# Packing the chunk operands of two RWKV heads into common tiles, with three scalings on another engine and more products of zeros at the start

## The chip, the cores and the metric

The kernel runs on one core of a Trainium2 chip. The metric is the time of one execution on the device in microseconds (us). A run is given as the median of several executions; the profile comes from one execution, taken by the hardware profiler.

## The reference, cut to what matters

The program is two layers of a decoder trunk on 256 tokens of width 1024. Each layer has a differential-attention branch and an RWKV-7 branch (8 heads of 64), then an output projection, a SwiGLU feed-forward part and a gated embedding. The change lies in the RWKV branch, whose core is a recurrence over tokens:

```
def step(state, inp):
    r_t, w_t, k_t, v_t, a_t, b_t = inp
    sa = jnp.einsum('bhvk,bhk->bhv', state, a_t)
    state = (state * w_t[:, :, None, :] + sa[..., None] * b_t[:, :, None, :]
             + v_t[..., None] * k_t[:, :, None, :])
    return state, jnp.einsum('bhvk,bhk->bhv', state, r_t)
...
yr = rwkv7_scan(rh, heads(decay), kh, vh, -kk, kk * ah)
```

All values are float32.

## The kernel before, in words

The kernel works in a transposed layout: channels lie on the 128 partitions, tokens along the free axis. Two heads of 64 channels share the 128 partitions, so a tensor of 512 channels is four pairs j (0 to 3) with heads e = 0 (partitions 0 to 63) and e = 1 (64 to 127). The 256 tokens of the recurrence are cut into four chunks c of 64, which makes 16 combinations of j and c.

**Two streams of work.** `main_g` is a generator with the layer's large products: the input projection, whose weights come by DMA and are split into a high part `wh` (ScalarE, L110) and a low part `wl` (VectorE, L111), the attention and its projection. The RWKV part is written out beside it and calls `fill(t)`, which lets `main_g` go on for an amount of TensorE time t taken from a table by name (`FP0`, `FP1`). The large products so stand between the small ones on TensorE, in an order fixed before the run. Tiles of one kind come from pools; the pool of 4 KB tiles (`slot`) holds NSLOT of them.

**The stage that makes the operands (L663 to L724).** From the decay come `Pd` and `Pi`. `NK` (L664) holds, for each j and c, two blocks of 64 columns: the scaled removal keys and the scaled keys. `RA` holds the removal vectors and the receptances; there are four such tiles, one for each head e and two pairs, and only 64 of the 128 partitions of each are written here (L677 to L679). L712 multiplies NK by RA for each head, 128x128 per chunk (the Gram products). Of each result, three pieces go by ScalarE to `AT` and `L2` (L720, L721), and two masked pieces by VectorE: one into the other 64 partitions of the `RA` tile (L722), one into `RK` (L723). The `SV` tile of a head holds the state on its own 64 partitions and the values v on the other 64 (L738), so that one product of 128 rows (L843) sums both. `UV` holds the solved updates and the values. `NT` is the transposed `NK` (L744, L745).

**The triangular solve (L765 to L828).** VectorE inverts the diagonal 16x16 blocks; the result is spread over the partitions by masks `p0` and `p1` into `ex` (L804, L805), transposed on VectorE (L806) and used in 64 + 64 small products (L818).

**The recurrence (L838 to L886).** For each chunk: `pz` (L843), products with the solve's blocks (L854, L861, L867), each followed by copies, then the new state (L876, L884, L885). After every second chunk come the outputs: L898 with the state, L903 with `RK` and `UV`.

**The start (L228 to L243).** NWARM products of zeros run on TensorE while the first inputs are loaded.

Matmuls of float32 are issued as two passes, so their counts in the trace are twice those of the code; transposes are one pass.

Of the kernel before, what the change touches and what calls it, by code (L numbers as in the profile page):

```python
# [25 lines left out]
NSLOT = 27  # L26
# [4 lines left out]
NWARM = 11  # L31
# [26 lines left out]
def trunk(ctx: ExitStack, tc: tile.TileContext, x_in, p_in, ws, par, lora, cst, fin, relb, onehot, out):  # L58
# [19 lines left out]
    def slot8(shape, dt=F32, s="s8"):  # L78
        return sp.tile(shape, dt, tag="s8", bufs=1, name=nm(s))
# [287 lines left out]
    def layer(l):  # L367
# [295 lines left out]
        RA = [[slot([P, 8, P], F32, "RA") for _ in range(2)] for _ in range(2)]  # L663
        NK = slot8([P, 16, 2, 64], F32, "NK")  # L664
# [3 lines left out]
        V.scalar_tensor_tensor(out=NK[:, :, 0], in0=pt16(nb), scalar=-0.5, in1=pt16(Pi), op0=ALU.mult, op1=ALU.mult)  # L668
        fill(fp['pre'])
        V.tensor_mul(NK[:, :, 1], pt16(kp), pt16(Pi))  # L670
        fill(fp['pre'])
        for jp in range(2):
            js = slice(2 * jp, 2 * jp + 2)
            for e in range(2):
                h = half[e]
                ra = RA[e][jp]
                A.copy(ra[h, :, 0:1], pt16(kn[:, js])[h, :, 0:1])  # L677
                V.tensor_mul(ra[h, :, 1:64], pt16(kn[:, js])[h, :, 1:64], pt16(Pd[:, js])[h, :, 0:63])
                V.tensor_mul(ra[h, :, 64:128], pt16(zr[:, js])[h], pt16(Pd[:, js])[h])  # L679
                fill(fp['pre'])  # L680
# [13 lines left out]
        RK = [slot([P, 16, 64], F32, "RK") for _ in range(2)]  # L694
# [8 lines left out]
        def mask4(h, lo):  # L703
            n = h.stop - h.start
            return mg[h, lo:lo + 64].unsqueeze(1).broadcast_to([n, 4, 64])

        for j in range(4):

            pgs = [psax(), psax()]
            for c in range(4):  # L710
                for e in range(2):
                    PE.matmul(pgs[e][:, c * P:(c + 1) * P], NK[half[e], 4 * j + c].rearrange("p a s -> p (a s)"),  # L712
                              RA[e][j // 2][half[e], 4 * (j % 2) + c], start=True, stop=True)
            for e in range(2):
                h, oh = half[e], half[1 - e]
                ra = RA[e][j // 2]
                pg = pgs[e]
                pg3 = pg.rearrange("p (i s) -> p i s", i=4)
                for b in range(2):
                    A.copy(AT[quar[2 * e + b], 4 * j:4 * j + 4], pg3[quar[b], :, quar[b]])  # L720
                A.copy(L2[quar[e], 4 * j:4 * j + 4, quar[e]], pg3[0:32, :, 32:64])  # L721
                V.tensor_mul(ra[oh, 4 * (j % 2):4 * (j % 2) + 4, 0:64], pg3[64:128, :, 0:64], mask4(half[1], 0))  # L722
                V.tensor_mul(RK[e][:, 4 * j:4 * j + 4], pg3[:, :, 64:128], mask4(slice(0, P), 64))  # L723
                fill(fp['g'])  # L724


        SV = [slot([P, 16, 64], F32, "SV") for _ in range(2)]
        UV = [slot([P, 16, 64], F32, "UV") for _ in range(2)]
        NT = [slot([P, 8, P], F32, "NT") for _ in range(2)]
        for tb in range(2):  # L730
# [4 lines left out]
            for r in range(2):  # L735
                c = 2 * tb + r
                for e in range(2):
                    A.copy(SV[e][half[1 - e], c::4], pv4[half[r], :, e])  # L738
                    A.copy(UV[e][64:128, c::4], pv4[half[r], :, e])
            fill(fp['vt'])  # L740
        for i4 in range(4):
            pn = psax()
            for i in range(4):
                PE.transpose(pn[:, i * P:(i + 1) * P], NK[:, 4 * i4 + i].rearrange("p a s -> p (a s)"), ident)  # L744
            A.copy(NT[i4 // 2][:, 4 * (i4 % 2):4 * (i4 % 2) + 4], pn.rearrange("p (i v) -> p i v", i=4))  # L745
            fill(fp['vt'])
# [55 lines left out]
        for tile_, src in ((Ds, DD.rearrange("p t s -> p s t")), (Dt, DD)):  # L802
            ex = tp.tile([P, 16, 32], F32, tag="g2", bufs=3, name=nm("ex"))
            V.tensor_scalar_mul(ex[:, :, 0:16], src, p0)  # L804
            V.tensor_scalar_mul(ex[:, :, 16:32], src, p1)  # L805
# [25 lines left out]
        for e in range(2):  # L831
            G.memset(SV[e][half[e], 0::4], 0.0)
# [5 lines left out]
        for c in range(4):  # L838
            ch = c // 2
            pz = psax()  # L840
            for j in range(4):
# [392 lines left out]
```

## Time and profile before

| what | value |
|---|---|
| runs, median (lowest to highest) | 910.44 us (908.72 to 911.51), 3 runs |
| the profiled execution, whole | 909.44 us |
| its span, first to last instruction | 907.6 us |
| TensorE (PE) busy | 887.8 us |
| VectorE (DVE) busy | 709.6 us |
| ScalarE (ACT) busy | 515.8 us |
| GpSimd (POOL) busy | 18.4 us |

A time measured outside the profiler is compared with the whole time of the profiled execution, which lies 1.84 us over its span. Matmuls are pipelined, and their ends are modelled, so a busy TensorE isn't TensorE at its peak: in a row with many matmuls the time from the start of one to the start of the next says what it costs. PEld is the loading of the stationary operand.

### The profile page before, as it was taken

How to read it: one execution, taken by the hardware profiler on the slowest of the kernel's cores; microseconds unless marked ns; L12 is line 12 of the kernel's file. 1: busy time of each engine (PE TensorE's matmuls, PEld its weight loads, DVE VectorE, ACT ScalarE, POOL GpSimd, SP SyncE). 2: the span in 40 equal slices, each digit the busy share in tenths (PEclk: the TensorE clock that was granted, in tenths of full speed). 3: DMA queues.
4: the chain of work that ended last, by engine and by line, in shares of the span. 5: the costliest groups of instructions: out<-in, count | busy, mean ns of one | idle time of the engine just before them, and what ended most of it. 6: DMA issues, size and time to landing. Idle time of an engine off the chain costs nothing.

```text
span 907.6 us, 17784 instructions
## 1 busy us (share of the span) xinstructions
PE 887.8 (98%) x7011; PEld 800.3 (88%) x7011; DVE 709.6 (78%) x1270; ACT 515.8 (57%) x956; POOL 18.4 (2%) x59
## 2 busy tenths in 40 slices
PE   8999989999999999999999999999999999999996
PEld 7988879899988888889999997989989888888885
DVE  6659977688988888766785996768788888886666
ACT  6475665544555555545567564665465555554444
POOL 0000000100000000000001000000000000000000
PEclk9999999999999999999999999999999999999998
DMA  8563423445666666666554344333665666666661
GB/s 283 190 219 131 140 75 106 126 153 165 208 186 187 188 186 190 198 186 194 170 162 136 107 135 136 95 111 105 185 188 174 195 188 187 190 201 186 192 191 47
DMA packets 42540, 149.47 MB, mean 165 GB/s; under 512 B 4911, under 2 KB 6488, under 8 KB 42328
## 3 DMA queue, kind: packets, MB, share of 16 engines
q1 hardware_dynamic: 41896, 147.87, 53.6%
q8 instruction: 55, 0.90, 0.4%
q10 hardware_dynamic: 560, 0.46, 0.2%
q14 instruction: 29, 0.24, 0.1%
HBM read 147.25 MB, written 2.63 MB: 165 GB/s over the span
## 4 chain that ended last, share of the span: by engine, by line
PE 90%; DVE 6%; ACT 2%; issue 1%; DMA 1%; ACTq 0%; POOL 0%; DVEq 0%; POOLq 0%
PE mm L142 21%; PE mm L128 11%; PE mm L144 10%; PE mm L130 10%; PE mm L129 10%; PE ax L142 8%; PE ax L144 4%; DVE wl L111 2%; ACT wh L110 1%; PE mm L166 1%; PE ax L712 1%; PE mm L167 1%; PE mm L168 1%; PE ax L818 1%; PE ax L843 1%
## 5 line engine op out<-in xcount | busy, mean ns | idle before, releaser
L110 ACT CAST wh<-raw 128x1024 fp32r<-128x1024 f32 (+1 forms) x269 | 280.7, 1046 | 297.0 <-PE mm L142 100.6
L111 DVE TENSOR_TENSOR wl<-raw,wh 128x1024 fp32r<-128x1024 f32 (+1 forms) x269 | 327.3, 1219 | 105.4 <-ACT wh L110 103.9
L128 PE MATMUL mm<-x,wh 128*128 128x256 f32 x704 | 204.1, 290 | 2.1 <-ACT wh L110 1.7
L130 PE MATMUL mm<-x,wl 128*128 128x256 f32 x704 | 202.0, 288 | 0.6 <-DVE wl L111 0.5
L129 PE MATMUL mm<-x,wh 128*128 128x256 f32 x704 | 200.6, 285 | 0.0
L128 PEld LDWEIGHTS mm<-x,wh 128*128 128x128 f32 x704 | 135.0, 192 | 6.2 <-ACT wh L110 2.2
L130 PEld LDWEIGHTS mm<-x,wl 128*128 128x128 f32 x704 | 134.9, 192 | 4.2 <-DVE wl L111 1.6
L129 PEld LDWEIGHTS mm<-x,wh 128*128 128x128 f32 x704 | 135.0, 192 | 1.1 <-issue 0.2
L142 PE MATMUL mm<-f,wh 128*128 128x512 f32 x352 | 97.5, 395 | 0.0
L142 PE MATMUL mm<-x,wh 128*128 128x512 f32 x320 | 87.5, 395 | 0.0
L142 PE MATMUL ax<-x,wh 128*128 128x512 f32 x320 | 87.3, 394 | 0.0
L142 PEld LDWEIGHTS mm<-f,wh 128*128 128x128 f32 x352 | 59.7, 189 | 7.6
L144 PEld LDWEIGHTS mm<-f,wl 128*128 128x128 f32 x352 | 55.1, 189 | 8.1
L142 PEld LDWEIGHTS ax<-x,wh 128*128 128x128 f32 x320 | 54.7, 189 | 7.3
L142 PEld LDWEIGHTS mm<-x,wh 128*128 128x128 f32 x320 | 54.7, 189 | 7.3
L144 PE MATMUL mm<-f,wl 128*128 128x256 f32 x352 | 57.2, 280 | 0.0
L144 PEld LDWEIGHTS ax<-x,wl 128*128 128x128 f32 x320 | 49.1, 189 | 6.8
L144 PEld LDWEIGHTS mm<-x,wl 128*128 128x128 f32 x320 | 49.1, 189 | 6.8
L144 PE MATMUL ax<-x,wl 128*128 128x256 f32 x320 | 50.9, 281 | 0.0
L144 PE MATMUL mm<-x,wl 128*128 128x256 f32 x320 | 50.9, 281 | 0.0
L142 PE MATMUL mm<-m,wh 128*128 128x512 f32 x128 | 35.3, 396 | 0.0
L956 DVE TENSOR_TENSOR xs<-xs,mm 128x256 f32<-128x256 f32 x64 | 26.3, 416 | 9.3 <-PE mm L144 8.7
(293 smaller groups left out, 1385.1 us busy)
## 6 DMA issues: line engine op xcount, KB each, us to landing
raw<-ws SPq DMA_DIRECT2D x267, 512.0 KB, 3.6
lora<-lora SPq DMA_DIRECT2D x2, 768.0 KB, 5.6
vr<-vd SPq DMA_DIRECT2D x1, 1536.0 KB, 9.4
bias<-vr SPq DMA_DIRECT2D x1, 1024.0 KB
out<-y SPq DMA_DIRECT2D x3, 256.0 KB, 2.1
raw<-ws SPq DMA_DIRECT2D x2, 256.0 KB, 4.6
xs<-x_in SPq DMA_DIRECT2D x1, 512.0 KB
pi<-p_in SPq DMA_DIRECT2D x2, 256.0 KB, 3.8
```

Source lines behind the costliest of these rows:

```text
L110: A.copy(wh, raw)
L111: V.tensor_sub(wl, raw, wh.bitcast(F32))
L128: PE.matmul(dst, lh, rh, start=first, stop=False, **kw)
L129: PE.matmul(dst, lh, rl, start=False, stop=False, **kw)
L130: PE.matmul(dst, ll, rh, start=False, stop=last, **kw)
L142: PE.matmul(pm, wh[:, i * P:(i + 1) * P], src[k + i][2], start=k + i == 0, stop=False, skip_group_check=True)
L144: PE.matmul(pm[:, 0:T], wl[:, i * P:(i + 1) * P], src[k + i][0], start=False, stop=k + i == nk - 1, skip_group_check=True)
L166: PE.matmul(dst, x[0][:, tk], wh, start=first, stop=False, skip_group_check=True)
L167: PE.matmul(dst, x[1][:, tk], wh, start=False, stop=False, skip_group_check=True)
L168: PE.matmul(dst, x[0][:, tk], wl, start=False, stop=last, skip_group_check=True)
L712: PE.matmul(pgs[e][:, c * P:(c + 1) * P], NK[half[e], 4 * j + c].rearrange("p a s -> p (a s)"), RA[e][j // 2][half[e], 4 * (j % 2) + c], s ...
L956: V.tensor_add(xs[:, n], xs[:, n], pm)
```

## The change

- `RA` becomes two tiles instead of four; each holds both heads of two pairs on all 128 partitions, made by one operation each instead of one per head.
- `NK` gets a third block, a copy of the first for head 0 (ScalarE), so that head 0 reads its two blocks in the order 1, 2 and head 1 in the order 0, 1.
- The two masked pieces of a Gram result become one operation over 128 columns into a new tile `MK`, and `RK` goes.
- The state lies in one tile `S` for both heads; the values are read from `UV` alone. So `pz` is the sum of two products of 64 rows (RA with S, MK with UV) instead of one of 128; for chunk 0, whose state is zero, only the second. The updates of the state are one operation for both heads.
- `NT` comes from 32 transposes of 64 partitions per layer instead of 16 of 128.
- Three of the four scalings into `ex` go from VectorE to ScalarE.
- 15 products of zeros instead of 11; 26 slots instead of 27; the tile of `NK` grows from 8 KB to 12 KB.

```
-NSLOT = 27
+NSLOT = 26
-NWARM = 11
+NWARM = 15
...
-        RA = [[slot([P, 8, P], F32, "RA") for _ in range(2)] for _ in range(2)]
-        NK = slot8([P, 16, 2, 64], F32, "NK")
+        RA = [slot([P, 8, P], F32, "RA") for _ in range(2)]
+        NK = slot12([P, 16, 3, 64], F32, "NK")
         nb = slot([P, 4, T], F32, "nb")
         V.scalar_tensor_tensor(out=nb, in0=th, scalar=1.0, in1=kn, op0=ALU.add, op1=ALU.mult)
         fill(fp['pre'])
         V.scalar_tensor_tensor(out=NK[:, :, 0], in0=pt16(nb), scalar=-0.5, in1=pt16(Pi), op0=ALU.mult, op1=ALU.mult)
+        A.copy(NK[0:64, :, 2], NK[0:64, :, 0])
+        nk = [NK[half[e], :, 1 - e:3 - e].rearrange("p i a s -> p i (a s)") for e in range(2)]
         fill(fp['pre'])
         V.tensor_mul(NK[:, :, 1], pt16(kp), pt16(Pi))
         fill(fp['pre'])
         for jp in range(2):
             js = slice(2 * jp, 2 * jp + 2)
-            for e in range(2):
-                h = half[e]
-                ra = RA[e][jp]
-                A.copy(ra[h, :, 0:1], pt16(kn[:, js])[h, :, 0:1])
-                V.tensor_mul(ra[h, :, 1:64], pt16(kn[:, js])[h, :, 1:64], pt16(Pd[:, js])[h, :, 0:63])
-                V.tensor_mul(ra[h, :, 64:128], pt16(zr[:, js])[h], pt16(Pd[:, js])[h])
-                fill(fp['pre'])
+            ra = RA[jp]
+            A.copy(ra[:, :, 0:1], pt16(kn[:, js])[:, :, 0:1])
+            V.tensor_mul(ra[:, :, 1:64], pt16(kn[:, js])[:, :, 1:64], pt16(Pd[:, js])[:, :, 0:63])
+            fill(fp['pre'])
+            V.tensor_mul(ra[:, :, 64:128], pt16(zr[:, js]), pt16(Pd[:, js]))
+            fill(fp['pre'])
...
-        RK = [slot([P, 16, 64], F32, "RK") for _ in range(2)]
+        MK = [[slot([P, 8, P], F32, "MK") for _ in range(2)] for _ in range(2)]
...
-                    PE.matmul(pgs[e][:, c * P:(c + 1) * P], NK[half[e], 4 * j + c].rearrange("p a s -> p (a s)"),
-                              RA[e][j // 2][half[e], 4 * (j % 2) + c], start=True, stop=True)
+                    PE.matmul(pgs[e][:, c * P:(c + 1) * P], nk[e][:, 4 * j + c],
+                              RA[j // 2][half[e], 4 * (j % 2) + c], start=True, stop=True)
...
-                    A.copy(AT[quar[2 * e + b], 4 * j:4 * j + 4], pg3[quar[b], :, quar[b]])
-                A.copy(L2[quar[e], 4 * j:4 * j + 4, quar[e]], pg3[0:32, :, 32:64])
-                V.tensor_mul(ra[oh, 4 * (j % 2):4 * (j % 2) + 4, 0:64], pg3[64:128, :, 0:64], mask4(half[1], 0))
-                V.tensor_mul(RK[e][:, 4 * j:4 * j + 4], pg3[:, :, 64:128], mask4(slice(0, P), 64))
+                    A.copy(AT[quar[2 * e + b], 4 * j:4 * j + 4], pg3[quar[2 - 2 * e + b], :, quar[b]])
+                A.copy(L2[quar[e], 4 * j:4 * j + 4, quar[e]], pg3[quar[2 - 2 * e], :, 32:64])
+                V.tensor_mul(MK[e][j // 2][:, 4 * (j % 2):4 * (j % 2) + 4], pg3, mg.unsqueeze(1).broadcast_to([P, 4, P]))
...
-        SV = [slot([P, 16, 64], F32, "SV") for _ in range(2)]
+        S = slot([P, 16, 64], F32, "S")
...
-                    A.copy(SV[e][half[1 - e], c::4], pv4[half[r], :, e])
-                    A.copy(UV[e][64:128, c::4], pv4[half[r], :, e])
+                    A.copy(UV[e][half[e], c::4], pv4[half[r], :, e])
...
-        for i4 in range(4):
-            pn = psax()
-            for i in range(4):
-                PE.transpose(pn[:, i * P:(i + 1) * P], NK[:, 4 * i4 + i].rearrange("p a s -> p (a s)"), ident)
-            A.copy(NT[i4 // 2][:, 4 * (i4 % 2):4 * (i4 % 2) + 4], pn.rearrange("p (i v) -> p i v", i=4))
-            fill(fp['vt'])
+        for jp in range(2):
+            pn = [psax(), psax()]
+            for i in range(8):
+                for e in range(2):
+                    PE.transpose(pn[e][:, i * 64:(i + 1) * 64], nk[e][:, 8 * jp + i], ident[half[e], half[e]])
+            for e in range(2):
+                A.copy(NT[jp][:, :, half[e]], pn[e].rearrange("p (i v) -> p i v", i=8))
+                fill(fp['vt'])
...
-            V.tensor_scalar_mul(ex[:, :, 0:16], src, p0)
-            V.tensor_scalar_mul(ex[:, :, 16:32], src, p1)
+            A.activation(ex[:, :, 16:32], src, AF.Copy, scale=p1)
+            if tile_ is Ds:
+                V.tensor_scalar_mul(ex[:, :, 0:16], src, p0)
+            else:
+                A.activation(ex[:, :, 0:16], src, AF.Copy, scale=p0)
             V.transpose(lanes(tile_), ex)
...
-        for e in range(2):
-            G.memset(SV[e][half[e], 0::4], 0.0)
...
+            if c > 0:
+                for j in range(4):
+                    for e in range(2):
+                        PE.matmul(four(pz)[half[e], j], RA[j // 2][half[e], 4 * (j % 2) + c, 0:64], S[half[e], 4 * j + c],
+                                  start=j == 0, stop=False, skip_group_check=True)
             for j in range(4):
                 for e in range(2):
-                    PE.matmul(four(pz)[half[e], j], RA[e][j // 2][:, 4 * (j % 2) + c, 0:64], SV[e][:, 4 * j + c],
-                              start=True, stop=True)
+                    PE.matmul(four(pz)[half[e], j], MK[e][j // 2][half[e], 4 * (j % 2) + c, 0:64], UV[e][half[e], 4 * j + c],
+                              start=c == 0 and j == 0, stop=j == 3, skip_group_check=True)
...
-                for e in range(2):
-                    h = half[e]
-                    if c > 0:
-                        V.tensor_add(S1[h], four(pS)[h], SV[e][h, c::4])
-                    V.tensor_mul(SV[e][h, c + 1::4], S1[h], PC[h, c::4].unsqueeze(2).broadcast_to([64, 4, 64]))
+                    V.tensor_add(S1, four(pS), S[:, c::4])
+                V.tensor_mul(S[:, c + 1::4], S1, PC[:, c::4].unsqueeze(2).broadcast_to([P, 4, 64]))
...
-                        PE.matmul(four(py[e])[half[cc % 2], j], RK[e][:, 4 * j + cc], UV[e][:, 4 * j + cc],
+                        PE.matmul(four(py[e])[half[cc % 2], j], MK[e][j // 2][:, 4 * (j % 2) + cc, 64:128], UV[e][:, 4 * j + cc],
```

## Rows read from the trace of the kernel before

**Rows 1.** The page's first part: busy us, share of the span, instructions.

```profile
PE 887.8 (98%) x7011; PEld 800.3 (88%) x7011; DVE 709.6 (78%) x1270; ACT 515.8 (57%) x956; POOL 18.4 (2%) x59
```

**Rows 2.** Busy time by stretch: us, engines (instructions), granted clock, DMA share, GB/s.

```profile
71.50:117.68 46.18, 42.72 (x306) 37.74 (x305) 45.05 (x83) 28.08 (x71) 0.94 (x3) 1.00 0.35 108
126.00:200.00 74.00, 73.77 (x865) 67.85 (x862) 54.82 (x118) 42.17 (x102) 3.95 (x8) 1.00 0.36 106
498.00:549.05 51.05, 48.40 (x381) 44.91 (x379) 49.47 (x84) 29.82 (x67) 0.63 (x2) 1.00 0.43 128
```

**Rows 3.** Busy time around the first L818 of either layer, and its timeline.

```profile
115.25:117.68 2.43, 0.28 (x3) 0.10 (x2) 2.43 (x6) 1.38 (x5) 0.00 (x0) 0.99 0.09 12
117.68:121.00 3.32, 3.32 (x135) 3.26 (x136) 3.16 (x6) 1.77 (x4) 0.44 (x2) 0.50 0.70 188
546.59:549.05 2.46, 0.39 (x3) 0.03 (x1) 2.46 (x7) 0.00 (x0) 0.00 (x0) 1.00 0.41 75
...
117.68 1.93 PE L818 MATMUL ax<-D,BT 32*32 32x32 f32 x128 [2.15 <-DVE sm L480]
...
549.05 1.28 PE L818 MATMUL ax<-D,BT 32*32 32x32 f32 x128 [2.07 <-DVE ex L805]
```

**Rows 4.** Chain that ended last, shares by line: 71.5 to 118, then 498 to 550.

```profile
by line: DVE wl L111 20.0%; issue 12.9%; DVE RA L679 5.4%; DVE RK L723 4.7%; DVE p L795 4.5%; DVE RA L678 4.1%; DVE RA L722 3.9%; DVE rk L687 2.8%; DVE kn L653 2.8%; DVE k L536 2.8%; ACT NT L745 2.7%; DVE NK L668 2.6%; DVE bo L755 2.6%; DVE
by line: PE mm L128 18.9%; PE mm L129 18.6%; PE mm L130 18.0%; PE ax L712 12.2%; DVE wl L111 4.5%; ACT SV L738 2.8%; ACT UV L739 2.5%; PE ax L744 2.1%; DVE p L795 2.1%; PE ax L651 2.1%; ACT wh L110 2.0%; DVE D L806 2.0%; ACT AT L720 2.0%; P
```

**Rows 5.** Timeline of VectorE, layer 0, at RA and masks: start us, us, what.

```profile
77.90 0.67 DVE L678 TENSOR_TENSOR RA<-kn,Pd 64x504 f32<-64x504 f32 x1
...
80.52 0.69 DVE L536 SCALAR_TENSOR_TENSOR q<-mm,bc 128x512 f32<-128x512 f32 x1
...
87.69 0.43 DVE L722 TENSOR_TENSOR RA<-ax,cs 64x256 f32<-64x256 f32 x1
...
90.27 0.68 DVE L536 SCALAR_TENSOR_TENSOR k<-mm,bc 128x512 f32<-128x512 f32 x1
```

**Rows 6.** Groups by form: busy us, mean ns; L629: ns least/median/most.

```profile
L755 DVE TENSOR_TENSOR bo<-zv,ax 128x512 f32<-128x512 f32 x4 | 2.7, 680 | 0.0
L804 DVE TENSOR_SCALAR ex<-DD,cs 128x256 f32<-128x256 f32 x2 | 0.8, 391 | 0.0
L720 ACT COPY AT<-ax 32x128 f32<-32x128 f32 x16 | 4.1, 255 | 3.0 <-PE ax L712 2.7
L738 ACT COPY SV<-ax 64x256 f32<-64x256 f32 x16 | 5.9, 368 | 0.2
L629 ACT ACTIVATE kk<-zk,pr x8: 493/497/547, 55.3 to 485.3; 128x256 f32<-128x256 f32 x8
```

**Rows 7.** Timeline of TensorE in the recurrence of layer 0; x counts passes.

```profile
126.47 0.69 PE L843 MATMUL ax<-SV,RA 128*64 128x64 f32 x16
...
129.01 0.68 PE L861 MATMUL ax<-W,L 64*64 64x64 f32 x8
...
147.62 0.68 PE L898 MATMUL ax<-SV,RA 64*64 64x64 f32 x16
148.24 1.15 PE L903 MATMUL ax<-UV,RK 128*64 128x64 f32 x32
```

**Rows 8.** Timeline of TensorE: Gram products of layer 1.

```profile
511.02 2.02 PE L712 MATMUL ax<-RA,NK 64*128 64x128 f32 x16
...
514.59 1.16 PE L712 MATMUL ax<-RA,NK 64*128 64x128 f32 x16
```

**Rows 9.** The start: timeline of TensorE, and busy time by stretch.

```profile
1.19 4.42 PE L233 MATMUL mm<-zw 128*128 128x512 bf16 x11 [1.19 <-DVE zw L230]
7.32 0.38 PE L128 MATMUL mm<-x,wh 128*128 128x256 f32 x1 [1.71 <-ACT wh L110]
...
8.40:11.80 3.40, 3.40 (x18) 3.40 (x17) 3.25 (x7) 3.40 (x8) 0.00 (x0) 0.50 1.04 414
11.80:14.00 2.20, 2.20 (x20) 2.20 (x19) 2.20 (x6) 2.20 (x8) 0.00 (x0) 0.99 1.03 412
```

More of the change, by code (lines that the diff above doesn't have):

```diff
@@ L76, in slot, with slot12 @@
         return sp.tile(shape, dt, tag="s", name=nm(s))
-    def slot8(shape, dt=F32, s="s8"):
-        return sp.tile(shape, dt, tag="s8", bufs=1, name=nm(s))
+    def slot12(shape, dt=F32, s="s12"):
+        return sp.tile(shape, dt, tag="s12", bufs=1, name=nm(s))
     def small(shape, dt=F32, tag="sm", bufs=8):
@@ L701, in layer @@
         mg = cs[:, K_MG:K_MG + P]
-        def mask4(h, lo):
-            n = h.stop - h.start
-            return mg[h, lo:lo + 64].unsqueeze(1).broadcast_to([n, 4, 64])
         for j in range(4):
@@ L711, in layer @@
                 for e in range(2):
-                    PE.matmul(pgs[e][:, c * P:(c + 1) * P], NK[half[e], 4 * j + c].rearrange("p a s -> p (a s)"),
-                              RA[e][j // 2][half[e], 4 * (j % 2) + c], start=True, stop=True)
+                    PE.matmul(pgs[e][:, c * P:(c + 1) * P], nk[e][:, 4 * j + c],
+                              RA[j // 2][half[e], 4 * (j % 2) + c], start=True, stop=True)
             for e in range(2):
[L715 to L718, printed above, removed]
+                pg3 = pgs[e].rearrange("p (i s) -> p i s", i=4)
                 for b in range(2):
-                    A.copy(AT[quar[2 * e + b], 4 * j:4 * j + 4], pg3[quar[b], :, quar[b]])
-                A.copy(L2[quar[e], 4 * j:4 * j + 4, quar[e]], pg3[0:32, :, 32:64])
-                V.tensor_mul(ra[oh, 4 * (j % 2):4 * (j % 2) + 4, 0:64], pg3[64:128, :, 0:64], mask4(half[1], 0))
-                V.tensor_mul(RK[e][:, 4 * j:4 * j + 4], pg3[:, :, 64:128], mask4(slice(0, P), 64))
+                    A.copy(AT[quar[2 * e + b], 4 * j:4 * j + 4], pg3[quar[2 - 2 * e + b], :, quar[b]])
+                A.copy(L2[quar[e], 4 * j:4 * j + 4, quar[e]], pg3[quar[2 - 2 * e], :, 32:64])
+                V.tensor_mul(MK[e][j // 2][:, 4 * (j % 2):4 * (j % 2) + 4], pg3, mg.unsqueeze(1).broadcast_to([P, 4, P]))
                 fill(fp['g'])
-        SV = [slot([P, 16, 64], F32, "SV") for _ in range(2)]
+        S = slot([P, 16, 64], F32, "S")
         UV = [slot([P, 16, 64], F32, "UV") for _ in range(2)]
@@ L863, in layer @@
             for e in range(2):
-                G.tensor_copy(UV[e][0:32, c::4], W1[quar[e]])
+                G.tensor_copy(UV[e][quar[2 - 2 * e], c::4], W1[quar[e]])
             fill(fp['w2'])
@@ L868, in layer @@
                           skip_group_check=True)
-            V.tensor_copy(UV[0][32:64, c::4], four(pw)[quar[2]])
-            A.copy(UV[1][32:64, c::4], four(pw)[quar[3]])
+            V.tensor_copy(UV[0][quar[3], c::4], four(pw)[quar[2]])
+            A.copy(UV[1][quar[1], c::4], four(pw)[quar[3]])
             fill(fp['u'])
@@ L897, in layer @@
                         if cc > 0:
-                            PE.matmul(four(py[e])[half[cc % 2], j], RA[e][j // 2][half[e], 4 * (j % 2) + cc, 64:128],
-                                      SV[e][half[e], 4 * j + cc], start=j == 0, stop=False, skip_group_check=True)
+                            PE.matmul(four(py[e])[half[cc % 2], j], RA[j // 2][half[e], 4 * (j % 2) + cc, 64:128],
+                                      S[half[e], 4 * j + cc], start=j == 0, stop=False, skip_group_check=True)
             for j in range(4):
```

## The prediction

> **What bounds the kernel now.** I read the page first: TensorE is busy for 98% of the span and VectorE for 78% [rows 1], so a TensorE-bound kernel at first sight. The stretches, layer by layer, say more [rows 2]. In the recurrence (126 to 200 us) TensorE is busy for 73.77 of 74 us: what it does there is paid in full, and what VectorE saves there is worth nothing. In the stretch before it, where the chunk operands are made and masked, it is the other way round: in layer 0 (71.5 to 117.68) VectorE is busy for 45.05 of 46.18 us and TensorE idles 3.46; in layer 1 (498 to 549.05) VectorE for 49.47 of 51.05, and TensorE idles 2.65. Most of that idle time lies in one place: before the products of L818 TensorE works 0.28 of 2.43 us in layer 0 and 0.39 of 2.46 in layer 1, while VectorE works all the time [rows 3]: the products wait for the transposed diagonal blocks of `ex`. The chain that ended last shows the same for layer 0, lines of VectorE from one end to the other; in layer 1 it is mixed, with 55% in three lines of TensorE's own products and 5% in ScalarE's copies of `SV` and `UV` [rows 4]. So the change is judged by two sums: what leaves VectorE before L818, and what comes to TensorE in the recurrence.
>
> **The parts that leave VectorE.** `RA`: the four operations of one pair of head pairs took 77.90 to 80.52, 2.62 us [rows 5]. They cover 64 partitions each; afterwards two cover 128 with the same 512 elements in each partition. An operation on 128 partitions and 512 elements took 680 ns (L755) [rows 6], as these do, so half goes: 1.31 us, twice a layer, 2.6 us.
> Masks: six operations took 87.69 to 90.27, 0.43 each [rows 5]; two for each head and group of four chunks, eight times a layer, are 6.9 us. Afterwards one of 128x512 from PSUM: 0.60 to 0.70 by L755's 680 ns, less overlap, 5.2 us. That saves 1.7. But each waits for three copies of ScalarE out of the same bank, 255 ns each (L720; L721's has the same shape) [rows 6], a pace of about 0.8 us: eight times 0.8 is 6.4, and 0.5 is saved. ScalarE can run ahead where VectorE is busy with `RA` and `rk`; I take 1.2.
> Scalings: an `ex` on VectorE takes 0.39 us [rows 6]. Ahead of the first transpose one of two goes to ScalarE, and runs beside the other: 0.35 saved. The second pair goes whole, two at 497 ns (L629's shape) in series on ScalarE; it is needed only for the second set of L818, behind TensorE's other products.
> The Trainium skill, "ScalarE: Activation LUTs", Rules for kernel authors, says of `mul` "Use VectorE, not ScalarE". The rows agree on the price, 497 against 391 ns, but VectorE is what everything waits for here; by the rule the 0.35 would be no saving, and the sum below 0.7 us worse over two layers.
> Together 2.6 + 1.2 + 0.35 = 4.2 us a layer. The bounds: 2.6 + 0.5 = 3.1 if the scalings bring nothing, less 1.2 if the second write of `NK` (VectorE) has to wait for ScalarE's new copy inside the same tile (1024 elements on 64 partitions, an estimate: L738 took 368 ns for 256 [rows 6], four times that is 1.5, and part of it passes while VectorE hands over), so 1.9; and 2.6 + 1.7 + 0.6 = 4.9 above. The trace has no two engines writing interleaved columns of one tile at once, so this wait can't be excluded; behind it on VectorE would stand `RA` and everything after.
>
> **What else is moved, at no cost on the path.** ScalarE gains the `NK` copy (at most 1.5) and three scalings (1.5) and loses eight `SV` copies of 368 ns [rows 6], 2.9 us: about even over a layer, but in layer 1, where these copies are on the chain [rows 4], lighter at the right place. The two memsets of GpSimd on `SV` go. In the recurrence five operations of 0.42 us a layer leave VectorE: hidden under TensorE's work. If that cover were gone they would be a gain, so nothing is risked. The pool has 26 slots for 27, the tiles of this stage 7 (RA 2, MK 4, S 1) for 8: the same room at the peak. `MK` asks for two slots more at its place, but its writer is VectorE, behind the last readers of `kn`, `Pd` and `zr`, which free slots; I take nothing, at worst 1 us.
>
> **What comes to TensorE.** For chunk 0 eight products of K=64 replace eight of K=128. For chunks 1 to 3 there are sixteen instead of eight. A product is two passes. Sixteen passes took 0.69 us with K=128 (L843) and 0.68 with K=64 (L898), 32 took 1.15 (L903) [rows 7]: chunk 0 costs the same, and each other chunk (1.15 - 0.69) = 0.46 more; three a layer, 1.38 us, all of it in the recurrence, where nothing hides it.
> The Gram products (L712) get cheaper. 16 passes took 2.02 us where the two heads' products ran one after the other and 1.16 where they ran side by side on the two halves of the array [rows 8]. Of four groups a layer two ran apart (in layer 0, 77 to 92 us, and in layer 1 alike), since the two `RA` of a pair were made one after the other. With one `RA` both heads are ready together: up to 1.7 us a layer.
> The transposes of `NK` become 32 of 64 partitions for 16 of 128. Side by side the 32 cost about what the 16 did; one after the other they add at most sixteen passes like those of L712 that ran apart (2.02 / 16 = 0.126 us, [rows 8]), 2 us. They lie before L818, where TensorE has slack; I take 0.
>
> **The sum.** In layer 0 TensorE can give 3.46 idle + 1.7 = 5.2, more than VectorE's 4.2: 4.2 is gained. In layer 1 it can give 2.65 + 1.7 = 4.3 and hardly follows; I take 3.8. Together 8.0, less 2 x 1.38 = 2.8: 5.2 us faster.
> Then the start. The 11 products of zeros (4.42 us from 1.19) end at 5.6; TensorE idles 1.71 us to 7.32 [rows 9]. The granted clock is 1.00 until 8.4, then 0.50 (1.2 GHz) until 11.8, then 1.00 (2.4 GHz). 18 products took 3.40 us at half clock, 20 took 2.20 at full [rows 9]: 0.189 against 0.110 each, 1.4 us lost, with no other wait on TensorE behind it. Four more products of zeros shorten the idle stretch by 0.9 (at full clock) to all of it. After 2.2 us of idle in layer 1 the clock stayed at 1.00, after as much in layer 0 it went to 0.50 [rows 3]; so 1.71 falls sometimes, and 0.8 I expect not to. They end before 7.4 in the worst case (15 x 0.40 from 1.19 is 7.2), so they delay nothing. I take 1.4; the other end is 0.
> The profiled execution took 909.44 us, 907.6 span and 1.84 around it. 909.44 - 5.2 - 1.4 = 902.8; that is 7.6 below the median of the runs, 910.44, of which 1.0 is the profiled execution's own distance. I say **902.8 us**.
>
> **Rivals.** *Better*: in layer 0 the idle stretch before L818 was followed by half clock: 1.93 us for the 128 passes against 1.28 in layer 1 [rows 3], and eight products of 256 columns behind them, some 0.65 more. If the stall shrinks enough, 1.3 us come on top: 901.5. For it speaks that the stall is VectorE's; against it that TensorE gets there earlier too.
> *The relief is half lost*: the write of `NK` waits for the copy, the masks go at ScalarE's pace and the scalings bring nothing: 1.9 a layer for 4.2 and 3.8. 3.8 - 2.8 + 1.4 = 2.4: 907.0; without the start's 1.4, 908.4. For it: ScalarE's three copies are as long as one new mask.
> *Slower*: the 64-row products don't run side by side. Eight passes on one half took 0.68 us (L861), as long as sixteen on two [rows 7]; chunk 0 then costs 0.5 more, chunks 1 to 3 some 1.4 each, 4.6 a layer instead of 1.38, and the transposes add 1 a layer beyond TensorE's slack. 8.0 + 1.4 - 2 x 5.6 = -1.8: 911.2. It decides once TensorE's extra work is over 4.7 us a layer. Against it: L898 and half of L712 do run side by side; for it: the other half of L712 doesn't, in the same program order.
>
> **Numbers.** Forecast 0.50, better 0.12, half lost 0.23, slower 0.15 (a third of it ending near no change). A change under 0.3% can't be told from none; the bound is 907.7. The forecast gives faster 0.48, same 0.02; better 0.12 faster; half lost 0.13 faster, 0.10 same; slower 0.05 same, 0.10 slower: 0.73, 0.17, 0.10. The likeliest case runs from 899 to 906 (1.9 to 4.9 a layer, the start at 0 or 1.4). The range runs from 899.0, which takes in the better case, to 909.0, past half lost without the start's gain; that leaves out the slower case and some below.
>
> **What would show it.** VectorE's busy time in the stretch before L818 falls by some 4 us a layer, with TensorE's idle time there not larger; four operations on `RA` of about 0.68 us and eight on `MK` of 0.60 to 0.70 a layer; L712 in four groups of 16 passes near 1.16 us; 32 passes of about 1.15 us before `Z` in chunks 1 to 3; granted clock 1.00 from 5 us on. I am wrong if VectorE waits at `NK` or `MK`, if the gap before L818 is as wide as now though VectorE is lighter, if the products of a pair come one after the other, or if half clock comes at another place.

## The result and the profile after

The changed kernel takes 898.84 us (median of 4 runs, 898.42 to 899.60) beside 909.58 us of the kernel before on the same chip: a ratio of 0.9888, 95% interval 0.9874 to 0.9901. That is 10.7 us faster where 6.6 to 7.6 were forecast, and 898.84 is 0.2 us below the low end of the stated range. The prediction counted from a median of 910.44; the ratio applied to that gives 900.2, inside the range. The profiled execution took 899.05 us with a span of 897.3, against 909.44 and 907.6.

The page's first part, of the kernel after, beside [rows 1]:

```profile
PE 882.9 (98%) x7143; PEld 796.0 (89%) x7143; DVE 694.5 (77%) x1230; ACT 515.1 (57%) x944; POOL 16.3 (2%) x55
```

VectorE lost 15.1 us of work (709.6 to 694.5), TensorE 4.9 although it has 132 instructions more. TensorE's idle time, span less busy time, fell from 19.8 to 14.4. So about half of the 10.3 us of span is idle time and half is TensorE's own work. The forecast's terms for that work, the start aside, nearly cancel: 2.8 more in the recurrence, up to 3.4 less in the Gram products.

The stretches before the first diagonal-block products (L817, L818 before) of layer 0 and layer 1 and the recurrence, as in [rows 2], and the 2.4 us just before those products, as in [rows 3] (us, busy us and instructions of TensorE, its weight loads, VectorE, ScalarE, GpSimd, granted clock, DMA share, GB/s):

```profile
71.50:108.76 37.26, 35.84 (x288) 31.78 (x287) 36.67 (x60) 24.39 (x55) 0.76 (x3) 1.00 0.41 123
118.40:191.50 73.10, 72.62 (x888) 66.54 (x887) 49.74 (x109) 41.15 (x99) 3.17 (x8) 1.00 0.36 105
498.00:537.66 39.66, 39.66 (x350) 36.97 (x348) 38.92 (x64) 27.10 (x58) 0.20 (x1) 1.00 0.43 126
...
106.33:108.76 2.43, 2.43 (x21) 2.30 (x21) 2.43 (x6) 1.42 (x3) 0.00 (x0) 1.00 0.71 216
535.20:537.66 2.46, 2.46 (x13) 1.75 (x11) 2.46 (x5) 1.47 (x2) 0.00 (x0) 1.00 0.38 80
```

The gap before the products is gone in both layers: TensorE works all the 2.4 us where it worked 0.3 and 0.4. In layer 1 it never idles in the whole stretch; there VectorE has stopped setting the pace, though it is busy for 38.92 of 39.66 us and has little to spare. In layer 0 it has not quite, as the waits of TensorE from 70 to 545 us show:

```profile
PE ax L817 <- ACT Q L822: 1.2, 1, 1.2
PE ax L710 <- DVE MK L718: 0.9, 1, 0.9
PE ax L710 <- DVE RA L680: 0.5, 1, 0.5
PE ax L857 <- ACT Z L849: 0.4, 1, 0.4
```

VectorE's timeline of layer 0 at the places of [rows 5]:

```profile
74.05 1.22 DVE L668 SCALAR_TENSOR_TENSOR NK<-nb,Pi 128x1024 f32<-128x1024 f32 x1
75.18 1.22 DVE L672 TENSOR_TENSOR NK<-kp,Pi 128x1024 f32<-128x1024 f32 x1
76.32 0.68 DVE L678 TENSOR_TENSOR RA<-kn,Pd 128x504 f32<-128x504 f32 x1
76.91 0.68 DVE L680 TENSOR_TENSOR RA<-zr,Pd 128x512 f32<-128x512 f32 x1
77.52 0.68 DVE L536 SCALAR_TENSOR_TENSOR q<-mm,bc 128x512 f32<-128x512 f32 x1
...
83.17 1.88 DVE L718 TENSOR_TENSOR MK<-ax,cs 128x512 f32<-128x512 f32 x3
84.96 0.68 DVE L536 SCALAR_TENSOR_TENSOR k<-mm,bc 128x512 f32<-128x512 f32 x1
```

A pair of `RA` takes 1.20 us (76.32 to 77.52) for 2.62. Three masks take 1.79, 0.60 each, without a wait between them. The two writes of `NK` follow one another without a gap.

TensorE's groups by line and shape, whole kernel (busy us, mean ns | idle time before them), first of the kernel before, then of the kernel after:

```profile
L712 PE MATMUL ax<-RA,NK 64*128 64x128 f32 x128 | 13.2, 282 | 1.0 <-DVE RA L679 0.7 <-ACT L L721 0.2
L843 PE MATMUL ax<-SV,RA 128*64 128x64 f32 x128 | 6.4, 229 | 0.0
L903 PE MATMUL ax<-UV,RK 128*64 128x64 f32 x128 | 5.5, 226 | 0.1
L876 PE MATMUL ax<-UV,NT 128*64 128x64 f32 x96 | 4.9, 229 | 0.0
L744 PE MATMUL ax<-cs,NK 128*128 128x128 f32 x32 | 4.5, 278 | 0.4 <-ACT wh L110 0.3
L898 PE MATMUL ax<-SV,RA 64*64 64x64 f32 x96 | 3.1, 223 | 0.0
```

```profile
L710 PE MATMUL ax<-RA,NK 64*128 64x128 f32 x128 | 9.5, 284 | 1.4 <-DVE MK L718 0.9 <-DVE RA L680 0.5
L879 PE MATMUL ax<-UV,NT 128*64 128x64 f32 x96 | 5.5, 230 | 0.0
L846 PE MATMUL ax<-UV,MK 64*64 64x64 f32 x128 | 5.2, 220 | 0.0
L903 PE MATMUL ax<-UV,MK 128*64 128x64 f32 x128 | 4.6, 225 | 0.0
L842 PE MATMUL ax<-S,RA 64*64 64x64 f32 x96 | 4.1, 224 | 0.0
L739 PE MATMUL ax<-cs,NK 64*128 64x64 f32 x64 | 3.0, 229 | 0.0
L898 PE MATMUL ax<-S,RA 64*64 64x64 f32 x96 | 2.8, 224 | 0.0
```

The mean of one product hardly differs; the busy time of the groups does, because overlapping products of a group count once. Gram products: 13.2 to 9.5. Transposes of `NK`: 4.5 to 3.0, though there are twice as many. Products for the output (L903, L898): 8.6 to 7.4; 1.0 of that lies in the last group of L903 of each layer, which took 1.67 us before and 1.15 after. Products for the new state (L876, L879 after): 4.9 to 5.5.

For `pz` the rows of L846 and L842 can't be added, since the two groups overlap. Timeline of TensorE, kernel after, chunk 1 of layer 0:

```profile
132.24 0.68 PE L842 MATMUL ax<-S,RA 64*64 64x64 f32 x16
132.75 0.63 PE L846 MATMUL ax<-UV,MK 64*64 64x64 f32 x16
```

Together they take 1.14 us, for 0.69 of L843 [rows 7]. Three such chunks and one group of 0.68 in each layer make 8.2 us, for the 6.4 of L843.

The granted clock was 0.50 from 8.4 to 11.8 and from 117.7 to 121.0 in the kernel before [rows 3, 9]. The profiled execution after has it at 1.00 through both places. In both kernels it is 0.50 again behind TensorE's last product, for the last 5 to 7 us, where it costs nothing.

### The profile page after: what moved, and what is told of

Read it like the earlier page. It is cut to its first block, busy times and chain, and to the rows that moved or that the text cites. A ratio compares the mean times of both kernels' runs of the same rounds, so it can differ in the third digit from the quotient of the medians.

```text
span 897.3 us, 17983 instructions
## 1 busy us (share of the span) xinstructions
PE 882.9 (98%) x7143; PEld 796.0 (89%) x7143; DVE 694.5 (77%) x1230; ACT 515.1 (57%) x944; POOL 16.3 (2%) x55
## 4 chain that ended last, share of the span: by engine, by line
PE 88%; DVE 6%; ACT 2%; issue 1%; DMA 1%; SPq 0%; POOL 0%; DVEq 0%; ACTq 0%; POOLq 0%
PE mm L142 20%; PE mm L128 11%; PE mm L144 10%; PE mm L130 10%; PE mm L129 10%; PE ax L142 8%; PE ax L144 4%; DVE wl L111 2%; PE mm L166 1%; ACT wh L110 1%; PE mm L168 1%; PE mm L167 1%; DMA raw<-ws 1%; PE ax L710 1%; DMA pi<-p_in 1%
## 5 line engine op out<-in xcount | busy, mean ns | idle before, releaser
L110 ACT CAST wh<-raw 128x1024 fp32r<-128x1024 f32 (+1 forms) x269 | 280.7, 1046 | 292.8 <-PE mm L142 99.6
```

The lines of the kernel that those rows point to most:

```text
L110: A.copy(wh, raw)
```

## The experiments

Each was timed in five rounds against the kernel before on its own chip. "Against after" is the difference of its ratio from 0.9888, times 909.6 us; the interval of a ratio is 0.8 to 1.3 us wide to either side, and the difference of two ratios is uncertain by some 1.7 us (an estimate, from two such intervals). Busy and idle time of TensorE (idle is span less busy) are those of the profiled executions; the last column is the span less that of the kernel after. The spans come from single executions on several chips, on which the kernel before had medians from 908.40 to 910.02 us.

| run | ratio to before, 95% interval | against after, us | TensorE busy / idle, us | span, us |
|---|---|---|---|---|
| before | 1 | +10.2 | 887.8 / 19.8 | +10.3 |
| after | 0.9888 [0.9874, 0.9901] | 0 | 882.9 / 14.4 | 0 |
| e1 eleven zeros | 0.9892 [0.9878, 0.9905] | +0.4 | 882.1 / 14.4 | -0.8 |
| e2 fifteen zeros alone (before) | 1.0004 [0.9995, 1.0013] | +10.6 | 888.2 / 17.9 | +8.8 |
| e3 heads apart | 0.9920 [0.9907, 0.9934] | +2.9 | 886.6 / 12.8 | +2.1 |
| e4 more rows in pz | 0.9924 [0.9910, 0.9937] | +3.3 | 884.8 / 14.4 | +1.9 |
| e5 chunk operands per head | 0.9975 [0.9965, 0.9984] | +7.9 | 888.3 / 15.7 | +6.7 |
| e6 masks in two | 0.9903 [0.9889, 0.9917] | +1.4 | 883.5 / 13.9 | +0.1 |
| e7 scalings on VectorE | 0.9908 [0.9895, 0.9922] | +1.8 | 883.9 / 15.2 | +1.8 |
| e8 VectorE as before | 0.9991 [0.9982, 0.9999] | +9.4 | 889.5 / 16.3 | +8.5 |
| e9 operands three times | 0.9961 [0.9949, 0.9973] | +6.6 | 885.7 / 19.5 | +7.9 |
| e10 state per head | 0.9896 [0.9882, 0.9909] | +0.7 | 883.2 / 14.8 | +0.7 |
| e11 block copy on VectorE | 0.9910 [0.9896, 0.9923] | +2.0 | 883.4 / 16.0 | +2.1 |
| e12 bonus behind blocks | 0.9920 [0.9907, 0.9932] | +2.9 | 884.8 / 16.1 | +3.6 |

**e1 and e2, the products of zeros.**

```diff
-NWARM = 15      (e1, in the kernel after)
+NWARM = 11
-NWARM = 11      (e2, in the kernel before)
+NWARM = 15
```

> The changed kernel with 11 products of zeros in place of 15, all else as changed. Theory (the four added products keep the clock at full level at the start): half clock comes back after the first products of weights, and the time is 1.4 us above the changed kernel's 898.8, so 900.2, 0.990 of before. Rival (the start gains nothing, the whole gain lies in the two layers): 898.8, 0.988. Rival 2 (the shorter stall before L818 and not the start decides about half clock in the whole run): as rival 1, with half clock neither at the start nor in layer 0.

> The kernel before with 15 products of zeros in place of 11, nothing else changed. Theory: the start's 1.4 us alone, 0.9985 of before, with half clock still behind the stall before L818 in layer 0. Rival: 1.000.

Neither moved the time by what its interval can tell. e2 is the direct test: +0.4 us, from -0.5 to +1.2, which leaves out a gain of 1.4. e1 can't decide by itself. In the profiled execution of e1 the 11 products left the clock at 1.00 all the same (timeline of TensorE, e1): the weights came earlier, and the idle time was 0.22 us, not 1.71 [rows 9].

```profile
1.19 4.88 PE L233 MATMUL mm<-zw 128*128 128x512 bf16 x11 [1.19 <-DVE zw L230]
6.29 0.45 PE L128 MATMUL mm<-x,wh 128*128 128x256 f32 x1 [0.22 <-ACT wh L110]
```

The first cast of weights (ScalarE, L110) began at 6.66 us in the profiled execution of the kernel before, at 5.63 in e1 and at 5.66 in that of the kernel after. So the full clock at the start of the kernel after need not be owed to the four added products: with weights as early, 11 were enough in e1. There the first product of weights began at 6.29; in the kernel after it stands right behind the 15 products of zeros and began at 6.78.

In e2 the clock was at 1.00 through the start too and 0.51 from 116.2 to 119.5, in layer 0, so the zeros do nothing for that place. The span of its profiled execution was 1.5 us shorter, as the step would have it, but the median of 11 runs was not. How often the start falls to half clock with 11 products can't be read from runs without a profile; that stays open.

**e3, the Gram products head after head.**

```diff
-            for c in range(4):
-                for e in range(2):
+            for e in range(2):
+                for c in range(4):
```

> The changed kernel with the Gram products of a group of four chunks issued head after head (8 passes, then 8) instead of alternating. VectorE and ScalarE have the same work. Theory 1 (VectorE sets the pace before L818, TensorE has slack there): under 1 us more, 899 to 900. Theory 2 (TensorE sets the pace there too, and heads side by side are a good part of the gain): four groups a layer at 2.02 for 1.16 us, 0.86 x 4 x 2 = 6.9 us more at most, 3 to 7 us, 902 to 906.

2.9 us slower, between its two theories. Timeline of TensorE in layer 1, e3, then the same group in the kernel after:

```profile
505.53 1.71 PE L710 MATMUL ax<-RA,NK 64*128 64x128 f32 x16
```

```profile
505.45 1.16 PE L710 MATMUL ax<-RA,NK 64*128 64x128 f32 x16
```

Four such groups in layer 1 are 2.2 us, the 2.1 that the span shows. The Gram products' busy time is 13.1 for 9.5, but idle time falls by 1.6 us: in layer 0 the longer products only fill waits. What the pairs save is paid out in full in layer 1 and hardly in layer 0.

**e4, eight more products in `pz`** for the chunks 1 to 3, with a tile of zeros, so that the sum is unchanged.

```diff
+                for j in range(4):
+                    for e in range(2):
+                        PE.matmul(four(pz)[half[e], j], RA[j // 2][half[e], 4 * (j % 2) + c, 0:64], zf[half[e]],
+                                  start=False, stop=False, skip_group_check=True)
```

> The changed kernel with eight more products of 64 rows in chunks 1 to 3 of the recurrence, RA with a tile of zeros, added into the same sum (48 passes a layer more; the result is the same). Theory (in the recurrence TensorE's time is paid in full): 0.46 us a chunk, three chunks, two layers, 2.8 us more, 901.6, 0.991. Rival (these products lie in gaps that TensorE has anyway): under 1 us more.

3.3 us by the ratios, 1.9 by the span, on either side of the theory's 2.8 and over the rival's 1. In its trace one added group takes 0.47 us (132.46 to 132.93 in layer 0), six of them 2.8. Most of what is added to TensorE in the recurrence is paid.

**e5, the chunk operands per head.**

```diff
-            V.tensor_mul(ra[:, :, 1:64], ...)
-            V.tensor_mul(ra[:, :, 64:128], ...)
+            for h in half:
+                V.tensor_mul(ra[h, :, 1:64], ...)
+                V.tensor_mul(ra[h, :, 64:128], ...)
```

> The kernel after, but each chunk operand is made in two operations of 64 partitions, one per head: four operations more on VectorE in each layer, some 0.65 us each. Theory 1 (VectorE's work before the diagonal-block products sets the time, as the prediction's sum has it): 2.6 us a layer come back, 5.2 in all, some 904, and TensorE idles that much more before those products. Theory 2 (VectorE has come to have slack there, TensorE's own products set the time): under 2 us in all. In both, the products of the two heads of a pair are then ready one after the other, which may bring up to 0.85 us more for each of two groups a layer; the trace tells that by the duration of the groups of 16 passes (1.2 against 2.0).

7.9 us slower, more than the 5.2 of theory 1; with the 0.85 us that the expectation allowed for each of four groups it comes to 8.6. TensorE's groups of e5, to be read beside those of the kernel after:

```profile
L710 PE MATMUL ax<-RA,NK 64*128 64x128 f32 x128 | 13.3, 284 | 0.8 <-DVE RA L680 0.5
L739 PE MATMUL ax<-cs,NK 64*128 64x64 f32 x64 | 4.3, 229 | 0.1
...
L817 PE MATMUL ax<-D,BT 32*32 32x32 f32 x256 | 2.6, 193 | 2.0 <-DVE D L805 2.0
```

Only 1.3 us of the loss is idle time; 5.4 is TensorE's own busy time, 3.8 of it in the Gram products and 1.3 in the transposes of `NK`. VectorE's four operations do two things: they make the products wait (2.0 us at L817 in layer 0), and they make the heads of a pair come apart again. In the program as compiled TensorE's stream then holds four products of one head and four of the other, in the first and the third group of each layer, where that of the kernel after alternates; the trace has the third group of layer 0 as eight passes at 83.41 and eight at 86.57, 1.16 us each. That this is the order in which the operands were expected to be ready is likely, but not shown. Nor does e5 tell what the heads coming apart cost from what VectorE's time costs: where TensorE waits for VectorE, longer products only take the place of waiting.

**e9, VectorE's time alone**: the second write of `NK` three times over, with the same values, so that VectorE loses as much and the heads' products stay alternating in all groups but one.

```diff
-        V.tensor_mul(NK[:, :, 1], pt16(kp), pt16(Pi))
+        for _ in range(3):
+            V.tensor_mul(NK[:, :, 1], pt16(kp), pt16(Pi))
```

> The kernel after, but the product that fills the second column block of the tile NK (128x1024, about 1.13 us from one to the next) is computed three times instead of once: some 2.3 us a layer more on VectorE, close to what the two operations for one on the chunk operands cost in the run before, while the instruction order of TensorE keeps the two heads' products alternating in all groups but one of layer 1. Theory 1 (VectorE sets the time in both layers): 4.5 us slower in all, some 903.5, half of it in each layer. Theory 2 (VectorE sets the time in layer 0 only, and in layer 1 it was the products of a pair coming apart that cost): some 2.3 in layer 0, under 1 in layer 1, 901 to 902. Theory 3 (the loss of the run before was the products coming apart in both layers): under 1 us.

6.6 us slower, beyond theory 1, in another way than e5: idle time grew by 5.1, busy time by 2.8. Timeline of TensorE, e9, at the first Gram products of layer 0 and at those of layer 1 that wait for a mask; below it busy time by stretch:

```profile
79.92 1.27 PE L711 MATMUL ax<-RA,NK 64*128 64x128 f32 x18 [2.81 <-DVE NK L673]
...
516.80 1.16 PE L711 MATMUL ax<-RA,NK 64*128 64x128 f32 x8 [1.08 <-DVE MK L719]
```

```profile
518.90:522.20 3.30, 3.30 (x23) 2.85 (x22) 3.30 (x5) 0.10 (x1) 0.00 (x0) 0.50 0.50 140
```

In layer 0 the 2.3 us come back one for one (2.81 for 0.55 of waiting). In layer 1 the products wait 1.1 us for a mask and 1.4 more before the diagonal-block products, and 2.0 us after the end of the first wait 3.3 us at clock 0.50 begin, which cost about half of that again. So theory 2 falls: layer 1 of the kernel after has no slack for VectorE either. The 4.5 us on VectorE come back as idle time, 5.1; the clock and the one group whose heads came apart are the rest.

**e6, e7 and e8, the other reliefs.**

```diff
-                V.tensor_mul(MK[e][j // 2][:, 4 * (j % 2):4 * (j % 2) + 4], pg3, ...)
+                for lo in (0, 64):
+                    V.tensor_mul(MK[e][j // 2][:, 4 * (j % 2):4 * (j % 2) + 4, lo:lo + 64], pg3[:, :, lo:lo + 64], ...)
...
-            A.activation(ex[:, :, 16:32], src, AF.Copy, scale=p1)
-            if tile_ is Ds:
-                V.tensor_scalar_mul(ex[:, :, 0:16], src, p0)
-            else:
-                A.activation(ex[:, :, 0:16], src, AF.Copy, scale=p0)
+            V.tensor_scalar_mul(ex[:, :, 0:16], src, p0)
+            V.tensor_scalar_mul(ex[:, :, 16:32], src, p1)
```

The first part is e6, the second e7; e8 is both, with the edit of e5.

> The kernel after, but each mask is made in two operations of 128x256 out of the same bank, for one of 128x512: eight operations more on VectorE in each layer. Two of 0.40 for one of 0.61 us would be 1.5 us a layer on VectorE. Theory 1 (VectorE sets the time): 2 to 3 us slower in all, some 901.5. Theory 2 (TensorE's own products set it, or ScalarE's three copies from the same bank do): under 1 us.

> The kernel after, but all four scalings of the inverted diagonal blocks run on VectorE again. Theory 1: 0.35 us a layer on the path, 0.7 us slower in all; the second pair, behind the first transpose, costs nothing. Theory 2: no difference, under 0.4 us. The rule that such products belong on VectorE would have it up to 0.7 us faster.

> The kernel after with all three reliefs of VectorE before the diagonal-block products taken back together: chunk operands per head, masks in two operations, scalings on VectorE. TensorE's products are those of the kernel after. Theory 1 (the relief sets the gain): 4.2 us a layer come back, 8 to 8.5 in all, some 907, and the idle stretch on TensorE before the diagonal-block products is over 2 us again, in layer 0 perhaps with the clock at 0.50 behind it. Theory 2 (most of the gain is TensorE's own, products of a pair side by side): 3 to 5 us in all, 902 to 904.

e6 can't be told from the kernel after: its interval overlaps, the span is 0.1 longer. Its masks (timeline of VectorE, layer 0):

```profile
82.84 2.07 DVE L719 TENSOR_TENSOR MK<-ax,cs 128x256 f32<-128x256 f32 x6
84.83 0.68 DVE L536 SCALAR_TENSOR_TENSOR k<-mm,bc 128x512 f32<-128x512 f32 x1
```

Six take 1.99 us, 0.33 from one to the next, where six of the kernel before took 2.58 [rows 5]. So two operations for one cost 0.06, not 0.19: e6 adds 0.5 us a layer to VectorE where 1.5 was meant, too little to decide between its theories. What the masks gained over the kernel before came only in part from their number: with e6's pace 0.5 us a layer, of 16 x 0.43 - 8 x 0.60 = 2.1.

e7 loses 1.8 us by its ratio, at the edge of what can be told, and 1.8 by its span; in the trace all of it comes before layer 1, whose first Gram product starts at 507.52 for 505.45. Its timeline of TensorE there, and a stretch behind it:

```profile
115.00 1.88 PE L814 MATMUL ax<-D,Q 32*32 32x32 f32 x128 [2.13 <-ACT Q L819]
```

```profile
115.00:118.60 3.60, 3.60 (x137) 3.54 (x138) 3.11 (x6) 1.72 (x3) 0.00 (x0) 0.53 0.69 164
```

The wait for the copy of `Q1` is 0.9 longer than the 1.2 of the kernel after, and half clock follows. The way goes through VectorE: its scalings push the softmax of the other branch back, ScalarE's exponentials (L477) begin at 110.97 for 110.31, and the copy stands behind them. The Trainium skill, "ScalarE: Activation LUTs", Rules for kernel authors, wants such products on VectorE; by e7's 1.8 us that is not the faster place here, since VectorE is the engine that the others wait for.

e8 loses 9.4 us, nearly the whole gain, as theory 1 has it. But the trace doesn't show it as idle time (1.9) so much as in TensorE's busy time (6.6), which theory 2 had named: 3.7 in the Gram products and 1.5 in the transposes, whose heads come apart as in e5. The waits before the first diagonal-block products are 1.4 us in layer 0 and 1.2 in layer 1, not over 2, and the clock stays at 1.00 there. So e8 takes back the time on VectorE and the pairing of the heads together; it doesn't part them.

**e10, the state per head in the recurrence.**

```diff
-                V.tensor_mul(S[:, c + 1::4], S1, ...)
+                for h in half:
+                    V.tensor_mul(S[h, c + 1::4], S1[h], ...)
```

(and the same for the addition ahead of it).

> The kernel after, but the state is updated per head, two operations of 64 partitions for one of 128: five operations of about 0.4 us more on VectorE in each layer, 2.1 us, all in the recurrence. The prediction's step says hidden under TensorE's work: no difference, under 0.4 us. The rival (the state's update is on the path from one chunk to the next) says 1.5 to 4 us slower.

0.7 us, within the interval, which reaches into the rival's range; VectorE's busy time rose from 694.5 to 699.2, by 4.7 us. So most of it is covered, as the step says. Not all: one new wait of TensorE in the recurrence, 0.5 us for the copy into `UV` (L905 on L873, layer 0), stands in the trace.

**e11 and e12, towards a faster one.**

```diff
-        A.copy(Q1, blocks(BT, Ds))
+        V.tensor_copy(Q1, blocks(BT, Ds))
```

e12 has that too, and the calls `bonus(0)` and `bonus(1)` behind the last `fill(fp['q1'])`.

> The kernel after, but the copy of Q1 out of PSUM (128x512, 0.56 us on ScalarE) runs on VectorE. In layer 0 of the kernel after TensorE waits 1.2 us for it, since ScalarE has other copies queued ahead of it, while VectorE idles 1.5 us at that place. Theory 1 (VectorE is what the stretch before the products waits for, any operation more there costs): 0.5 to 1.2 us slower. Theory 2 (after the change the wait has gone over to ScalarE there): 0.5 to 1.2 us faster.

> The kernel after, with the Q1 copy on VectorE and the two products of the bonus term (0.68 us each on VectorE, wanted only at the end of the recurrence) moved from before the diagonal-block products to behind them. Theory 1 (VectorE's work before those products sets the time): up to 1.4 us a layer faster beyond the copy's effect, 896 or less. Theory 2 (layer 1 has no idle time of TensorE left there, layer 0 only 1.2 us): 1 us or less faster in all, 898.

Both are slower: e11 by 2.0 us, the way of its theory 1 but more than its 1.2, e12 by 2.9, against both of its theories. TensorE's timeline of layer 0, e11, then e12:

```profile
115.76 1.30 PE L817 MATMUL ax<-D,Q 32*32 32x32 f32 x128 [2.68 <-DVE Q L822]
```

```profile
106.21 1.28 PE L814 MATMUL ax<-D,BT 32*32 32x32 f32 x128 [0.60 <-DVE D L802]
...
110.73 1.29 PE L814 MATMUL ax<-D,Q 32*32 32x32 f32 x128 [1.62 <-DVE Q L819]
```

In e11 the copy stands on VectorE behind the softmax of the other branch, and the wait is 2.7 us for 1.2. In e12 the products do start 2.55 us earlier (106.21 for 108.76), and the time is not kept: between the two sets of layer 0 TensorE has 13 products of the other stream (1.6 us) where the kernel after has 24 (3.1 us), so it waits at both sets, in layer 1 as well (0.2 and 1.3 us there). In both the clock falls to 0.50 for some 3 us, beginning 1.4 and 1.8 us after the end of the longest wait. No run's ratio is below that of the kernel after.

## Why the prediction was right, and where its sum was not

**What bounds the kernel** was read rightly. Taking VectorE's relief back, and with it the pairing of the heads, costs 9.4 of the 10.2 us (e8). Adding 4.5 us to VectorE alone before the diagonal-block products costs 6.6, half clock and one pair coming apart included (e9), while 4.7 us added to it in the recurrence cost 0.7, within the interval (e10), and products added to TensorE there are paid, 3.3 for 2.8 (e4).

**The relief** of 4.2 and 3.8, TensorE's idle time and the Gram products together, came within 0.4 us of the forecast, with its parts shared out otherwise. TensorE's idle time in the layers fell by about 3.9: the stretches had 3.46 and 2.65 and 0.8 at the second set of products, and keep 1.42 in layer 0 and the two later waits of 1.2 and 0.4. The Gram products gave 13.2 - 9.5 = 3.7. Together 7.6 for 8.0. `RA` was 2.84 a layer for 2.6. The masks were 2.1 for 1.2: VectorE sat idle before none of them, so they don't wait for ScalarE's copies, and the six before were slower than their size (last section). What the scalings gave isn't measured by itself; taking them back lost 1.8 (e7), half clock included. The prediction took the Gram products as slack for TensorE. They are also a gain of their own where TensorE sets the pace: lengthened alone, they cost 2.1 us of span, all of it in layer 1 (e3).

**The recurrence** cost 8.2 - 6.4 = 1.8 us for a forecast of 2.8. The price of one added group was right, 1.14 - 0.69 = 0.45 for 0.46, and e4's 0.47 confirms it. But the 0.69 was read from a group in one piece; three of the eight groups of L843 came in two pieces (in layer 0, 0.33 us at 176.35 and 0.68 at 176.93), which those of the kernel after do not.

**The steps that were mis-sized.** "I take 0" for the transposes of `NK`: they lost 1.5 us over both layers (4.5 to 3.0): with the heads alternating, twice as many of half the size took less time, not the same. With the heads apart, in e5 and e8, the same transposes took 4.3 and 4.5. The products for the output were not in the sum at all: 1.2 us less, for the same count; the new state's were not either, 0.6 more. The *better* rival's step happened as well: no half clock behind L817 in layer 0, which that rival priced at 1.3. With the 1.0 us of the recurrence these make 4.4 us that the forecast has not. By place: the first Gram product of layer 1 starts at 505.45 for 511.02 [rows 8], so 5.6 of the 10.3 us lie before it and 4.7 behind it, where the sum had 4.2 and 2.4.

**The start** fails: 1.4 taken, no gain by e2, and none seen by e1. In the profiled pair a gain is there, but the weights came 1.0 us earlier in the execution after, so it may be luck. (The idle time in layer 1 that the prediction gives as 2.2 us in this step is 2.07 in its row.) The sum for that pair, -7.6 + 1.8 + 0.6 - 1.5 - 1.2 - 1.3 - 1.4, is -10.6, beside the -10.3 of the spans. Without the start's 1.4 it is -9.2, for 10.2 by the ratio and 10.7 by the medians, so 1.0 to 1.5 us of them are not accounted for, about the width of the interval. The copies of `SV`, the memsets and the slots were not run by themselves.

**The range.** The bounds that the prediction names, 1.9 to 4.9 a layer and the start at 0 or 1.4, add up to 901.0 to 908.4, not to 899 to 906, and the *better* case on top to 899.7. So the measured 898.84 lies beyond its own sums; that the stated range comes within 0.2 us of it is luck in part.

**The rivals.** *Half lost* is out: VectorE's second write of `NK` began at 75.18, right behind the first, and ran beside ScalarE's copy (75.30 to 76.35) without growing longer (1.22 us); the masks followed one another at 0.60. *Slower* is out too: the 64-row products ran side by side wherever the heads alternated. What the rival feared, for the Gram products and the transposes, is what e3 and e5 make by hand, at 2.9 and 7.9 us, the latter with VectorE's time in it.

## What to carry to other kernels

When two halves of an array can work at once, see that their operands become ready together: here one operation over both halves let the products of a pair alternate, which saved 3.7 us of TensorE in the Gram products and 1.5 in the transposes beside the time on VectorE. Judge an edit on an engine with slack by the engine that waits for it, stretch by stretch, and take the products that change shape into the sum too, even where they lie in slack, for the slack may be gone afterwards. Starting a step earlier gains nothing where no other work is left to stand in its waits (e12).

## What the runs showed of the hardware that was not expected

A wait of TensorE has a second price, and it can't be read from the wait's length. Half clock (0.50) for about 3.4 us followed waits of 2.15 us (before, layer 0), 2.1 (e7), 2.7 (e11), 1.6 (e12), and 1.1 (e9, layer 1), at once in the first two, 1.4 and 1.8 us after the wait in the next two and 2.0 in the last. The clock stayed at 1.00 after 2.07 (before, layer 1), 2.0 (e5, layer 0), 2.8 (e9, layer 0) and 1.2 (after). Which of them is followed by it the runs don't settle.

An operation of VectorE that begins on other partitions than the one before it starts later. Timeline of VectorE in e5, the chunk operands of one pair, the heads in turn:

```profile
75.96 0.67 DVE L679 TENSOR_TENSOR RA<-kn,Pd 64x504 f32<-64x504 f32 x1
76.55 0.68 DVE L680 TENSOR_TENSOR RA<-zr,Pd 64x512 f32<-64x512 f32 x1
77.26 0.68 DVE L679 TENSOR_TENSOR RA<-kn,Pd 64x504 f32<-64x504 f32 x1
77.86 0.69 DVE L680 TENSOR_TENSOR RA<-zr,Pd 64x512 f32<-64x512 f32 x1
78.58 0.69 DVE L536 SCALAR_TENSOR_TENSOR q<-mm,bc 128x512 f32<-128x512 f32 x1
```

From one operation to the next it is 0.59 and 0.60 us within a head, 0.71 and 0.72 where the half changes: there the next begins only as the last ends. The masks of the kernel before read from partition 64 and from partition 0 in turn, and went at 0.44 to 0.46 for 256 elements; only the last of the six, which like the operation after it begins at partition 0, was followed 0.35 after its start (89.92 to 90.27 [rows 5]). Those of e6, which all begin at partition 0, go at 0.33. The Trainium skill, "VectorE: DVE Perf Modes", Two Vector instructions with no wait between them, has this as a model: an instruction whose input or output starts in another group of 32 partitions than the last one of that memory is held until every earlier one has finished. These rows agree. For sixteen masks a layer it is 16 x 0.10 = 1.6 us, an estimate from these paces and more than the 0.9 by which the masks' term was short.
